# Reading the gate tiles ahead and moving two heads' scaling in a hybrid conv, gated linear attention and SwiGLU block

## The chip, the cores and the metric

The kernel runs on one core of one Trainium2 chip. The time is the device time of one execution in microseconds (us). Of the kernel before, three executions were timed, and one more was profiled. A difference of 0.2% is about 2.3 us here.

## The reference

`x` has 512 rows of 1024 values, in float32. One layer is computed:

```python
x = x + 0.5 * swiglu(rmsnorm(x, norm_ffn1_g), ffn1_w_gu, ffn1_w_down)
x = x + hybrid_mixer(rmsnorm(x, norm_mix_g), w_in, conv_w, ...)
x = x + 0.5 * swiglu(rmsnorm(x, norm_ffn2_g), ffn2_w_gu, ffn2_w_down)
return rmsnorm(x, final_norm_g)
```

The change touches the mixer:

```python
cb, cc, cu, q, k, v, g_lr, r, ga, gb = split(h @ w_in)
y_conv = (cb * causal_short_conv(cc * cu, conv_w)) @ w_out_conv
log_a = log_sigmoid(g_lr @ gate_w_up + gate_b) / 16
o = gla_chunked(q, k, v, log_a)                      # four heads, chunks of 64 rows
y_gla = (rmsnorm_of_each_head(o) * gla_norm_g * silu(r)) @ w_out_gla
merged = sigmoid(ga) * y_conv + sigmoid(gb) * y_gla
return merged @ w_o
```

`ga` and `gb` are the two gates, 512 x 1024 each. The attention is cut into chunks; in each, `q` and `k` are scaled by exponentials of cumulated decays, the scores are formed, a state is carried on, and the output is made of both.

## The kernel before, in words

**Products.** Each float32 weight tile is split into a high part (`wh`, a cast on ACT, L380) and the rest (`wl`, a subtraction on DVE, L381), and each operand likewise (L668, L669). A product takes three matmuls: high by high, high by low, low by high. The larger products are made by a scheme with seven half-size products in place of eight: the steps m1, p2, q6, p5, q7, p3 and p4. In a "tall" product (`Tall`, matmuls in L696) each step has two halves of 12 matmuls of 512 columns; in a "set" (`Set`, L613) a step has 24 matmuls of 256 columns. The program emits PE's instructions in a fixed order, step after step.

**Feeding PE.** `Weights.issue` (L351 to L389) is called some two steps ahead of PE. It loads the tiles of a step from HBM (SP's queue, L343, 512 KB, into 10 buffers `f`), adds tiles to one another where the scheme wants sums (DVE L359 and L374, or an accumulating DMA from POOL's queue, L347), and splits them into `wh` and `wl`, three buffers each. So a step can begin once its cast on ACT and its subtraction on DVE are done.

**Emptying PE.** Results stand in banks. A set has a bank "b" to which m1, q6, q7 and p4 add in turn; after m1, q6 and q7 it is copied out by ACT (L618), and the next of these steps can only begin to write it when that copy is done. A tall's banks are emptied by ACT (L1467) and DVE (L1469).

**The mixer.** PE takes `q`, `k`, then the tall products `v`, `ga`, `gb`, then eight sets (four for the convolution, 0 to 3; two for `cb`, 4 and 5; two for `r`, 6 and 7), then the tall product "out" (`w_out_conv`), `w_out_gla` (`mm_wide`, L449 to L451), and `w_o`. Each tile of `ga` and `gb` goes to HBM when it is made (L1484). The attention of the four heads is threaded between: a table `hooks` names after which step of PE each part of a head is emitted. The parts are `gates` (cumulated decays), `decays` (two subtractions, DVE L1336 and L1339), `exps` (ACT L1345 to L1349), `scale`, `scale_k`, `scale_q` (multiplications, all in the helper `mul`, DVE L583), `scores` (PE L1385, L1387, L1398), `state` (PE L1410, ACT L1412, DVE L1414), `output` (PE L1427 and L1430, ACT L1433 and L1435, DVE L1436) and `squares`. A hook gives the place in the program; the scheduler then orders DVE, ACT, POOL and SP by its own estimate of when things are ready. On each engine, instructions run strictly in that order, and one that waits holds all behind it.

**The gates' way back.** `gate(name, t, e)` (L1684) loads a gate tile (128 x 512, 256 KB, SP's queue, L1686) into one of the six buffers `tp` and takes its sigmoid on ACT (L1687). All sixteen loads stand around the `w_out_gla` product: `between(e)` multiplies the `ga` tiles into the conv output (DVE L583), and after each half of the product the `gb` tiles are multiplied with the banks and added (L583, L1726).

**Tiles that the change uses.** `E`, `M`, `KS`, `EX`, `QS` are the five work tiles of a head, `G_tile(0)` to `G_tile(4)`; `sc` holds the masked scores. `YS` holds the convolution's output in 1024-column quarters, `two(0)` to `two(3)`, and is read by the operands of "out" (`co`, L655, L668, L669).

**The start.** `WARM` matmuls of ones (L277) run on PE before the first weights and inputs have come; each is recorded as two matmuls.

Of the kernel before, what the change touches and what calls it, by code (L numbers as in the profile page):

```python
# [11 lines left out]
AF = mybir.ActivationFunctionType  # L12
# [15 lines left out]
NTB = S // P  # L28
# [6 lines left out]

V_G1, V_GM, V_G2, V_GLA, V_CONV, V_GB = 0, 8, 16, 24, 32, 56
NVEC = 60
WARM = 10
ODD_FILL = 272

TAIL = 4
# [191 lines left out]
def block_kernel(ctx: ExitStack, tc: tile.TileContext, xT, vecs, gf, gup, wgl, wts, out):  # L233
# [25 lines left out]
    def T(dtype=F32):  # L259
        return tile_of("tp", [P, S], dtype)  # L260
# [321 lines left out]
    def mul(out_, a, b, eng=None):  # L582
        (eng or nc.vector).tensor_tensor(out=out_, in0=a, in1=b, op=ALU.mult)  # L583
# [608 lines left out]
    def mixer(norm, nxt):  # L1192
# [15 lines left out]
        def two(i):  # L1208
            return flat(i).rearrange("p (e t) -> p e t", e=2)
# [6 lines left out]
        def G_tile(i, dtype=F32):  # L1216
            cnt[0] += 1
            return pools["g"].tile([P, S], dtype, tag=f"g{i}", name=f"g{i}_{cnt[0]}")
# [100 lines left out]
        def gates(h):  # L1319

            a = AUX()
            nc.tensor.matmul(a, gup_w[:R3, h * DK : (h + 1) * DK], glr[:R3],
                             start=True, stop=True)
            b = vec[:, V_GB + h : V_GB + h + 1]
            nc.scalar.activation(E, a, AF.Abs, bias=b)
            nc.vector.tensor_scalar(out=M, in0=a, scalar1=b, scalar2=0.0,
                                    op0=ALU.add, op1=ALU.min)
            nc.scalar.activation(E, E, AF.Exp, scale=-1.0)
            nc.scalar.activation(E, E, AF.Ln, bias=1.0)
            nc.vector.tensor_tensor(out=M, in0=M, in1=E, op=ALU.subtract)  # L1330
            nc.vector.tensor_tensor_scan(out=E, data0=reset, data1=M, initial=0.0,
                                         op0=ALU.mult, op1=ALU.add)
# [21 lines left out]
        def scale(h):  # L1354

            q_, k_ = QK[h][:, 0], QK[h][:, 1]
            ref = sm4[:, 0]
            mul(q_, EX, q_)  # L1360
            mul(KX, pairs(KS)[:, :, 0], pairs(k_)[:, :, 0])
            mul(QX, pairs(q_)[:, :, 1], bc(ref[:, :, 1]))

        def scale_k(h):

            k_, dc = QK[h][:, 1], sm4[:, 1]
            mul(pairs(KS)[:, :, 1], pairs(KS)[:, :, 1], pairs(k_)[:, :, 1])
            mul(k_, M, k_)
            mul(pairs(KS)[:, :, 0], KX, bc(dc[:, :, 1]))

        def scale_q(h):

            q_ = QK[h][:, 0]
            ref, dc = sm4[:, 0], sm4[:, 1]
            mul(pairs(QS)[:, :, 1], QX, bc(dc[:, :, 0]))
            mul(pairs(QS)[:, :, 0], pairs(q_)[:, :, 0], bc(ref[:, :, 0]))
            mul(d2s, dc[:, :, 0], dc[:, :, 1])

        def scores(h):
# [14 lines left out]
            n = NTB - 1  # L1394
            tr = AUX()
            for t in range(n):
                b = slice(t * P, (t + 1) * P)
                nc.tensor.transpose(tr[:, b], KS[:, b], ident)  # L1398
            nc.scalar.copy(E[:, : n * P], tr[:, : n * P])

        def state(h):

            v = vt[h // 2]
            kvs = []
            for t in range(NTB - 1):
                if t % 2 == 0:
                    kv = AUX()
                hc = slice((t % 2) * DV, (t % 2) * DV + DV)
                kvs.append(kv[:, hc])
                nc.tensor.matmul(kvs[t], E[:, t * P : (t + 1) * P],  # L1410
                                 v[t][:, (h % 2) * DV : (h % 2) * DV + DV], start=True, stop=True)
            nc.scalar.copy(ST[0], kvs[0])  # L1412
            for t in range(1, NTB - 1):
                nc.vector.scalar_tensor_tensor(out=ST[t], in0=ST[t - 1], scalar=d2s[:, t : t + 1],  # L1414
                                               in1=kvs[t], op0=ALU.mult, op1=ALU.add)
# [114 lines left out]
        def split_o(h):  # L1530
            for a, b in split_pair(O[h]):
                og_h.append(a)
                og_l.append(b)

        hooks = {
            ("v", 0, "q6"): [decays, exps], ("v", 1, "p5"): [lambda: scale(0)],
            ("v", 0, "q7"): [lambda: scale_k(0)],
# [1 line left out]
            ("ga", 1, "m1"): [lambda: state(0)], ("ga", 1, "p2"): [lambda: output(0)],  # L1539
            ("ga", 0, "p5"): [lambda: squares(0)], ("ga", 1, "p5"): [lambda: gates(1)],  # L1540
            ("ga", 0, "q7"): [decays], ("ga", 1, "q7"): [exps],
            ("ga", 0, "p3"): [lambda: scale(1)], ("ga", 1, "p3"): [lambda: scale_k(1)],
            ("gb", 0, "m1"): [lambda: scores(1)], ("gb", 1, "m1"): [lambda: scale_q(1)], ("gb", 0, "p2"): [lambda: state(1)],
            ("gb", 1, "q6"): [lambda: output(1)], ("gb", 1, "q7"): [lambda: squares(1)],
            ("gb", 0, "p3"): [move], ("gb", 1, "p3"): [lambda: gates(2)],
            ("gb", 0, "p4"): [decays], (0, "p2"): [exps], (0, "q6"): [lambda: scale(2)],
            (0, "p5"): [lambda: scale_k(2)], (0, "q7"): [lambda: scale_q(2)],
            (0, "p3"): [lambda: scores(2)], (1, "q6"): [lambda: state(2)],
            (1, "q7"): [lambda: output(2)], (1, "p4"): [lambda: squares(2)],
            (1, "p3"): [lambda: gates(3)], (2, "p5"): [decays], (2, "q7"): [exps],  # L1550
            (3, "m1"): [lambda: scale(3)], (2, "p4"): [lambda: scale_k(3)],
            (2, "p3"): [lambda: scale_q(3)],
            (3, "q6"): [lambda: scores(3)], (3, "p3"): [lambda: state(3)],
            (4, "q6"): [lambda: output(3)], (4, "p3"): [lambda: squares(3)],
            (5, "q7"): [lambda: normalise(0)], (5, "p3"): [lambda: normalise(1)],
            (6, "q7"): [lambda: normalise(2)], (6, "p3"): [lambda: normalise(3)],
            ("out", 1, "p5"): [lambda: co.make("p4")], ("out", 0, "q7"): [lambda: split_o(0)],
            ("out", 1, "q7"): [lambda: split_o(1)], ("out", 0, "p3"): [lambda: split_o(2)],
            ("out", 1, "p3"): [lambda: split_o(3)],
        }  # L1560
# [121 lines left out]
        finish_late()  # L1682

        def gate(name, t, e):  # L1684
            g = T()
            tc.keep_in_program_order(nc.sync.dma_start(g, gates_d[name][2 * t + e]))  # L1686
            nc.scalar.activation(g, g, AF.Sigmoid)  # L1687
            return g

# [17 lines left out]
        def between(e):  # L1707
            def extra(k):
                if e == 1 and k == 3:
                    XS.append(big("X2"))  # L1710
                    x[:] = [XS[-1][:, k] for k in range(KD)]
                    for k_ in range(KD):
                        nc.gpsimd.dma_start(x[k_], xs[k_])
                if k in (1, 3, 4, 6):
                    t = (1, 3, 4, 6).index(k)
                    mul(m[e][t], m[e][t], gate("ga", t, e))
                if e == 1 and k in (5, 6):
                    turned(2 * (k - 5))
            return extra
# [91 lines left out]
```

## Time and profile before

| what | value |
|---|---|
| executions, not profiled | 1168.29, 1169.42, 1169.52 us; median 1169.42 us |
| the profiled execution | 1169.12 us, of which the span of the profile is 1167.4 us |
| granted TensorE clock | 0.999 |
| busy: PE, DVE, ACT, POOL | 1158.9, 895.1, 657.3, 127.4 us |
| HBM read and written | 124.55 and 8.39 MB |
| DMA loads of weights (SP's queue) | 219 of 512 KB |

The profile's times are from the start of the span. In a row of the timeline stand the start, the length, engine, line, operation, output and inputs, and in brackets how long the engine had been idle and what ended that. DVE and ACT begin an instruction slightly ahead of the recorded end of the one before, so that the distance between two starts is the price of the first: 1.14 us for a subtraction L381 of 128 x 1024, 0.60 us for an operation of 128 x 512, 0.34 us for one of 128 x 256. PE's matmuls overlap in the records; the distance between starts, 0.227 us for 512 columns and 0.12 us for 256, is what one costs.

### The profile page before, as it was taken

How to read it: one execution, taken by the hardware profiler on the slowest of the kernel's cores; microseconds unless marked ns; L12 is line 12 of the kernel's file. 1: busy time of each engine (PE TensorE's matmuls, PEld its weight loads, DVE VectorE, ACT ScalarE, POOL GpSimd, SP SyncE). 2: the span in 40 equal slices, each digit the busy share in tenths (PEclk: the TensorE clock that was granted, in tenths of full speed). 3: DMA queues.
4: the chain of work that ended last, by engine and by line, in shares of the span. 5: the costliest groups of instructions: out<-in, count | busy, mean ns of one | idle time of the engine just before them, and what ended most of it. 6: DMA issues, size and time to landing. Idle time of an engine off the chain costs nothing.

```text
span 1167.4 us, 16527 instructions
## 1 busy us (share of the span) xinstructions
PE 1158.9 (99%) x6428; PEld 1010.3 (87%) x6428; DVE 895.1 (77%) x1066; ACT 657.3 (56%) x832; POOL 127.4 (11%) x167
## 2 busy tenths in 40 slices
PE   9999999999999999999999999999999999999997
PEld 7888888989988888889999998888888888888886
DVE  7985666889887976777797999555876666799966
ACT  6565555634452756475654577525655556575543
POOL 0101110001120110110110112000101101101100
PEclk9999999999999999999999999999999999999999
DMA  9667786657665485878576787834567966877711
GB/s 363 129 183 165 170 219 162 173 131 175 170 207 153 96 223 152 209 208 215 134 174 155 181 205 213 288 109 131 118 181 163 231 171 157 203 176 165 184 48 72
DMA packets 59870, 203.22 MB, mean 174 GB/s; under 512 B 6960, under 2 KB 7088, under 8 KB 59792
## 3 DMA queue, kind: packets, MB, share of 16 engines
q0 software_dynamic: 20288, 73.41, 33.3%
q1 hardware_dynamic: 36912, 124.27, 32.4%
q10 hardware_dynamic: 2592, 4.49, 1.0%
q8 instruction: 50, 0.82, 0.3%
q14 instruction: 28, 0.23, 0.1%
HBM read 124.55 MB, written 8.39 MB: 114 GB/s over the span
## 4 chain that ended last, share of the span: by engine, by line
PE 95%; DVE 2%; ACT 1%; DMA 1%; issue 0%; SPq 0%; ACTq 0%; DVEq 0%
PE mm L696 48%; PE mm L613 23%; PE mm L432 5%; PE mm L408 3%; PE mm L410 3%; PE mm L409 3%; PE aux L840 1%; PE mm L451 1%; PE mm L450 1%; PE mm L449 1%; PE mm L1083 1%; PE mm L1082 1%; PE mm L1081 1%; PE aux L1427 1%; DVE wl L381 1%
## 5 line engine op out<-in xcount | busy, mean ns | idle before, releaser
L380 ACT CAST wh<-f 128x1024 fp32r<-128x1024 f32 (+1 forms) x349 | 365.5, 1049 | 361.3 <-PE mm L696 138.0
L381 DVE TENSOR_TENSOR wl<-f,wh 128x1024 fp32r<-128x1024 f32 (+1 forms) x349 | 424.1, 1217 | 181.2 <-ACT wh L380 180.4
L696 PE MATMUL mm<-wh,op 128*128 128x512 f32 x1680 | 528.1, 391 | 0.0
L696 PEld LDWEIGHTS mm<-wh,op 128*128 128x128 f32 x1680 | 315.5, 188 | 65.8 <-ACT tp L814 0.8
L696 PE MATMUL mm<-wl,op 128*128 128x512 f32 x840 | 327.3, 390 | 0.2 <-DVE wl L381 0.2
L613 PE MATMUL mm<-op,wh 128*128 128x256 f32 x1456 | 263.7, 284 | 0.2 <-ACT tp L618 0.2
L613 PEld LDWEIGHTS mm<-op,wh 128*128 128x128 f32 x1456 | 227.0, 191 | 1.1 <-ACT tp L618 0.4
L347 POOL DMA_DIRECT2D f<-f x132 | 113.8, 865 | 910.5 <-DVE wl L381 434.1
L613 PE MATMUL mm<-op,wl 128*128 128x256 f32 x728 | 206.1, 283 | 0.3 <-DVE wl L381 0.3
L696 PEld LDWEIGHTS mm<-wl,op 128*128 128x128 f32 x840 | 157.8, 188 | 32.6 <-DVE wl L381 1.0
L613 PEld LDWEIGHTS mm<-op,wl 128*128 128x128 f32 x728 | 139.1, 191 | 0.5 <-DVE wl L381 0.5
L668 ACT CAST op<-hid 128x1024 fp32r<-128x1024 f32 x42 | 44.0, 1050 | 23.2 <-PE mm L696 11.0
L669 DVE TENSOR_TENSOR op<-hid,op 128x1024 fp32r<-128x1024 f32 x42 | 51.1, 1217 | 2.9 <-ACT op L668 2.9
L408 PE MATMUL mm<-op,wh 128*128 128x512 f32 x132 | 51.4, 389 | 0.0
L409 PE MATMUL mm<-op,wh 128*128 128x512 f32 x132 | 51.4, 389 | 0.0
L410 PE MATMUL mm<-op,wl 128*128 128x512 f32 x132 | 51.4, 389 | 0.0
L432 PE MATMUL mm<-op,wh 128*128 128x512 f32 x192 | 48.3, 393 | 0.3 <-ACT wh L380 0.2
L374 DVE TENSOR_TENSOR f<-f,f 128x1024 f32<-128x1024 f32 x30 | 36.6, 1220 | 10.9 <-DMA f<-f 8.6
L432 PEld LDWEIGHTS mm<-op,wh 128*128 128x128 f32 x192 | 35.6, 188 | 8.8 <-ACT wh L380 1.1
L408 PEld LDWEIGHTS mm<-op,wh 128*128 128x128 f32 x132 | 24.8, 188 | 5.2
L409 PEld LDWEIGHTS mm<-op,wh 128*128 128x128 f32 x132 | 24.8, 188 | 5.2
L410 PEld LDWEIGHTS mm<-op,wl 128*128 128x128 f32 x132 | 24.8, 188 | 5.1
(326 smaller groups left out, 1194.8 us busy)
## 6 DMA issues: line engine op xcount, KB each, us to landing
f<-wts SPq DMA_DIRECT2D x219, 512.0 KB, 4.3
f<-f POOLq DMA_DIRECT2D x132, 512.0 KB, 5.1
X<-xT SPq DMA_DIRECT2D x8, 256.0 KB, 5.7
xs<-X POOLq DMA_DIRECT2D x8, 256.0 KB, 2.8
ga<-tp ACTq DMA_DIRECT2D x8, 256.0 KB, 5.2
gb<-tp ACTq DMA_DIRECT2D x8, 256.0 KB, 3.9
tp<-ga SPq DMA_DIRECT2D x8, 256.0 KB, 5.1
X<-xs POOLq DMA_DIRECT2D x8, 256.0 KB, 7.3
```

The source lines that it names most:

```text
L347: nc.gpsimd.dma_start(out_, a, accum_op=ALU.add)
L374: nc.vector.tensor_tensor(out=a11, in0=a11, in1=a22, op=ALU.subtract)
L380: nc.scalar.copy(h[:, :w], raw[:, :w])
L381: nc.vector.tensor_tensor(out=l[:, :w], in0=raw[:, :w], in1=h[:, :w].bitcast(F32), op=ALU.subtract)
L408: nc.tensor.matmul(o, wh, ah, start=first, stop=False)
L409: nc.tensor.matmul(o, wh, al, start=False, stop=False)
L410: nc.tensor.matmul(o, wl, ah, start=False, stop=last)
L432: nc.tensor.matmul(o[c], w[:, s : s + P], a[k], start=k == 0 and j == 0, stop=k == kt - 1 and j == 2)
L613: nc.tensor.matmul(to, ww[:, s], aa[:, t], start=fresh and k == 0 and e == 0 and j == 0, stop=k == 3 and j == 2, skip_group_check=True)
L668: nc.scalar.copy(hv, v)
L669: nc.vector.tensor_tensor(out=lv, in0=v, in1=hv.bitcast(F32), op=ALU.subtract)
L696: nc.tensor.matmul(self.bank[b][e], aa[:, c], ww, start=fresh and i == 0 and n == 0, stop=k == 3 and n == 2, skip_group_check=True)
```

## The change

Four things are changed.

1. **Four `ga` tiles of the first half** (e = 0) are loaded into `KS`, `EX`, `QS` and `sc` after the first half of m1 of "out" in the program (`fetch_gates`), and their sigmoid is taken after q6 (`open_gates`). The scheduler puts these loads further ahead, to where head 3 has read these tiles for the last time.
2. **Eight more** (`gb` of e = 0, `ga` of e = 1) are loaded into the quarters of `YS` within "out" (`fetch_more`); `gate` then takes a tile from there. The four `gb` tiles of e = 1 go through `tp` as before.
3. **Heads 1 and 3**: some of `decays`, `exps`, `scale`, `scale_k`, `scale_q`, `scores` and `state` hang on a later step.
4. `WARM` is 9 in place of 10.

```diff
-WARM = 10
+WARM = 9
...
+        ahead = {}
+        def fetch_gates():
+            for t, g in enumerate((G_tile(2), G_tile(3), G_tile(4), sc)):
+                nc.sync.dma_start(g, gates_d["ga"][2 * t])
+                ahead[t] = g
+        def open_gates():
+            for t in range(NTB):
+                nc.scalar.activation(ahead[t], ahead[t], AF.Sigmoid)
+        def fetch_more(name, e):
+            for t in range(NTB):
+                g = two(2 * e + t // 2)[:, t % 2]
+                nc.sync.dma_start(g, gates_d[name][2 * t + e])
+                ahead[name, t, e] = g
...
-            ("ga", 0, "p3"): [lambda: scale(1)], ("ga", 1, "p3"): [lambda: scale_k(1)],
+            ("ga", 1, "p3"): [lambda: scale(1)], ("ga", 1, "p4"): [lambda: scale_k(1)],
...
+            ("out", 0, "m1"): [fetch_gates], ("out", 1, "q6"): [open_gates],
+            ("out", 0, "q7"): [lambda: split_o(0), lambda: fetch_more("gb", 0)],
+            ("out", 0, "p4"): [lambda: fetch_more("ga", 1)],
...
         def gate(name, t, e):
-            g = T()
-            tc.keep_in_program_order(nc.sync.dma_start(g, gates_d[name][2 * t + e]))
+            g = ahead.get((name, t, e))
+            if g is None:
+                g = T()
+                tc.keep_in_program_order(nc.sync.dma_start(g, gates_d[name][2 * t + e]))
             nc.scalar.activation(g, g, AF.Sigmoid)
             return g
...
-                    mul(m[e][t], m[e][t], gate("ga", t, e))
+                    mul(m[e][t], m[e][t], ahead[t] if e == 0 else gate("ga", t, e))
```

The order that the scheduler makes of it is shown at three places. In the rows, the numbers are buffers; `g_536` to `g_540` are `E`, `M`, `KS`, `EX`, `QS`; the change's buffers are numbered one lower.

**DVE, head 1**, where `ga` ends and `gb` begins; `y` holds this head's `q` and `k`. Before:

```order
L381 TENSOR_TENSOR wl_4201<-f_3801,wh_4200 128x1024
L583 TENSOR_TENSOR y_3223<-g_539_3456,y_3223 128x512
L583 TENSOR_TENSOR g_538_3455<-g_538_3455,y_3223 128x4x64
L583 TENSOR_TENSOR g_539_3456<-g_538_3455,y_3223 128x256
L583 TENSOR_TENSOR g_539_3456<-y_3223,sm 128x256
L381 TENSOR_TENSOR wl_4221<-f_3851,wh_4220 128x1024
L1469 SCALAR_TENSOR_TENSOR tp_4082<-mm_4086,tp_4082 128x512
L1469 SCALAR_TENSOR_TENSOR tp_4084<-mm_4087,tp_4084 128x512
L583 TENSOR_TENSOR y_3223<-g_537_3454,y_3223 128x512
L583 TENSOR_TENSOR g_538_3455<-g_539_3456,sm 128x4x64
L381 TENSOR_TENSOR wl_4244<-f_4143,wh_4243 128x1024
```

The same place in the change:

```order
L381 TENSOR_TENSOR wl_4200<-f_3800,wh_4199 128x1024
L583 TENSOR_TENSOR y_3222<-g_539_3455,y_3222 128x512
L583 TENSOR_TENSOR g_538_3454<-g_538_3454,y_3222 128x4x64
L381 TENSOR_TENSOR wl_4217<-f_3850,wh_4216 128x1024
L1469 SCALAR_TENSOR_TENSOR tp_4081<-mm_4085,tp_4081 128x512
L1469 SCALAR_TENSOR_TENSOR tp_4083<-mm_4086,tp_4083 128x512
L583 TENSOR_TENSOR g_539_3455<-g_538_3454,y_3222 128x256
L583 TENSOR_TENSOR g_539_3455<-y_3222,sm 128x256
L381 TENSOR_TENSOR wl_4240<-f_4142,wh_4239 128x1024
L583 TENSOR_TENSOR y_3222<-g_537_3453,y_3222 128x512
L381 TENSOR_TENSOR wl_4258<-f_4191,wh_4257 128x1024
```

The second L381 now stands ahead of two 128 x 256 multiplications, and the third ahead of the multiplication of `k` and of one more 128 x 256.

**DVE, head 3**, in the last convolution set; `y` is the convolution's, `vec` its weights. Before:

```order
L1579 SCALAR_TENSOR_TENSOR tp_5308<-y_3223,vec,tp_5308 128x512
L1581 SCALAR_TENSOR_TENSOR y_3223<-y_3223,vec,tp_5304 128x512
L1581 SCALAR_TENSOR_TENSOR y_3223<-y_3223,vec,tp_5308 128x512
L1336 TENSOR_TENSOR g_537_3454<-g_536_3453 128x512
L1339 TENSOR_TENSOR g_538_3455<-g_536_3453 128x512
L381 TENSOR_TENSOR wl_5323<-f_4786,wh_5322 128x1024
L1593 SCALAR_TENSOR_TENSOR tp_5352<-mm_5274,tp_5350 128x512
L381 TENSOR_TENSOR wl_5361<-f_5042,wh_5360 128x1024
```

In the change, whose lines are numbered 21 higher here:

```order
L1600 SCALAR_TENSOR_TENSOR tp_5307<-y_3222,vec,tp_5307 128x512
L1602 SCALAR_TENSOR_TENSOR y_3222<-y_3222,vec,tp_5303 128x512
L1602 SCALAR_TENSOR_TENSOR y_3222<-y_3222,vec,tp_5307 128x512
L381 TENSOR_TENSOR wl_5320<-f_4785,wh_5319 128x1024
L1336 TENSOR_TENSOR g_537_3453<-g_536_3452 128x512
L1339 TENSOR_TENSOR g_538_3454<-g_536_3452 128x512
L1614 SCALAR_TENSOR_TENSOR tp_5349<-mm_5273,tp_5347 128x512
L381 TENSOR_TENSOR wl_5355<-f_5041,wh_5354 128x1024
```

The two subtractions of `decays` went behind one L381; the next L381 has the same work ahead of it as before.

**ACT, after head 3's output.** `O` and `aux` are the head's output and its bank, `tp` what is copied out of a set's bank. Before:

```order
L1433 ACTIVATE O<-aux_5792,vec 128x512
L1435 ACTIVATE g_538_3455<-aux_5792 128x512
L380 CAST wh_5849<-f_5320 128x1024
L380 CAST wh_5883<-f_5579 128x1024
L618 COPY tp_5877<-mm_5617 128x512
L380 CAST wh_5914<-f_5316 128x1024
```

In the change, where L1544 is `open_gates`:

```order
L1433 ACTIVATE O<-aux_5791,vec 128x512
L1435 ACTIVATE g_538_3454<-aux_5791 128x512
L1544 ACTIVATE sc<-sc 128x512
L380 CAST wh_5848<-f_5317 128x1024
L1544 ACTIVATE g_997_6690<-g_997_6690 128x512
L1544 ACTIVATE g_995_6688<-g_995_6688 128x512
L380 CAST wh_5882<-f_5578 128x1024
L618 COPY tp_5876<-mm_5616 128x512
L380 CAST wh_5913<-f_5313 128x1024
```

Three sigmoids (`sc`; `g_997`, which is `QS`'s tile; `g_995`, which is that of `KS`) now stand among the casts and copies of the sets, each behind its load. The fourth, in the tile of `EX`, stands some steps earlier, together with a load of ACT's function table.

More of the change, by code (lines that the diff above doesn't have):

```diff
@@ L1541, in mixer @@
             ("ga", 0, "q7"): [decays], ("ga", 1, "q7"): [exps],
-            ("ga", 0, "p3"): [lambda: scale(1)], ("ga", 1, "p3"): [lambda: scale_k(1)],
-            ("gb", 0, "m1"): [lambda: scores(1)], ("gb", 1, "m1"): [lambda: scale_q(1)], ("gb", 0, "p2"): [lambda: state(1)],
+            ("ga", 1, "p3"): [lambda: scale(1)], ("ga", 1, "p4"): [lambda: scale_k(1)],
+            ("gb", 1, "m1"): [lambda: scores(1)], ("gb", 0, "p2"): [lambda: scale_q(1)],
+            ("gb", 1, "p2"): [lambda: state(1)],
             ("gb", 1, "q6"): [lambda: output(1)], ("gb", 1, "q7"): [lambda: squares(1)],
@@ L1549, in mixer @@
             (1, "q7"): [lambda: output(2)], (1, "p4"): [lambda: squares(2)],
-            (1, "p3"): [lambda: gates(3)], (2, "p5"): [decays], (2, "q7"): [exps],
-            (3, "m1"): [lambda: scale(3)], (2, "p4"): [lambda: scale_k(3)],
+            (1, "p3"): [lambda: gates(3)], (2, "q7"): [decays], (3, "m1"): [exps],
+            (2, "p4"): [lambda: scale(3)], (3, "p2"): [lambda: scale_k(3)],
             (2, "p3"): [lambda: scale_q(3)],
@@ L1556, in mixer @@
             (6, "q7"): [lambda: normalise(2)], (6, "p3"): [lambda: normalise(3)],
-            ("out", 1, "p5"): [lambda: co.make("p4")], ("out", 0, "q7"): [lambda: split_o(0)],
+            ("out", 0, "m1"): [fetch_gates], ("out", 1, "q6"): [open_gates],
+            ("out", 1, "p5"): [lambda: co.make("p4")],
+            ("out", 0, "q7"): [lambda: split_o(0), lambda: fetch_more("gb", 0)],
+            ("out", 0, "p4"): [lambda: fetch_more("ga", 1)],
             ("out", 1, "q7"): [lambda: split_o(1)], ("out", 0, "p3"): [lambda: split_o(2)],
```

## The prediction

> **What bounds the kernel now.** I read the page first, then PE's waits, then the busy time by stage, then the timeline of PE and DVE around each wait. The page's busy times:
>
> ```profile
> PE 1158.9 (99%) x6428; PEld 1010.3 (87%) x6428; DVE 895.1 (77%) x1066; ACT 657.3 (56%) x832; POOL 127.4 (11%) x167
> ```
>
> PE is idle for 1167.4 - 1158.9 = 8.5 us of the span, and a part of that is the start and the tail after the last product. A change that leaves PE its products can therefore win only what PE waits for. The view of waits, for PE, names three in the middle of the program (the first number is the total in us):
>
> ```profile
> PE mm L613 <- DVE wl L381: 0.3, 1, 0.3
> PE mm L696 <- DVE wl L381: 0.2, 1, 0.2
> ...
> PE mm L613 <- ACT tp L618: 0.2, 1, 0.2
> ```
>
> Two are for a `wl` from DVE, one for a copy by ACT. The busy time by stage, for "out" and then for the `w_out_gla` product (start:end, length, then busy us of PE, PEld, DVE, ACT and POOL):
>
> ```profile
> 697.20:735.30 38.10, 38.10 (x170) 31.54 (x169) 34.92 (x36) 26.73 (x31) 6.88 (x11) 1.00 0.83 246
> 735.30:773.40 38.10, 38.10 (x170) 31.49 (x169) 17.88 (x21) 16.39 (x23) 0.00 (x0) 1.00 0.64 221
> ```
>
> PE is busy for all of both. The gate tiles stand in the second stage now and in the first and before it afterwards; no wait of PE stands where they are taken away.
>
> **Head 1's scaling.** The timeline of PE, then of DVE, where `ga` passes into `gb`:
>
> ```profile
> 474.05 0.61 PE L696 MATMUL mm<-wh,op 128*128 128x512 f32 x2
> ...
> 474.73 0.61 PE L696 MATMUL mm<-wh,op 128*128 128x512 f32 x2
> ...
> 475.92 0.62 PE L696 MATMUL mm<-wh,op 128*128 128x512 f32 x2
> ```
>
> ```profile
> 469.44 0.68 DVE L583 TENSOR_TENSOR y<-g,y 128x512 f32<-128x512 f32 x1
> 470.04 0.75 DVE L583 TENSOR_TENSOR g<-g,y 128x256 f32<-128x256 f32 x2
> 470.71 0.41 DVE L583 TENSOR_TENSOR g<-y,sm 128x256 f32<-128x256 f32 x1
> 471.05 1.21 DVE L381 TENSOR_TENSOR wl<-f,wh 128x1024 fp32r<-128x1024 f32 x1
> 472.19 1.27 DVE L1469 SCALAR_TENSOR_TENSOR tp<-mm,tp 128x512 f32<-128x512 f32 x2
> 473.38 0.67 DVE L583 TENSOR_TENSOR y<-g,y 128x512 f32<-128x512 f32 x1
> 473.98 0.41 DVE L583 TENSOR_TENSOR g<-g,sm 128x256 f32<-128x256 f32 x1
> 474.32 1.21 DVE L381 TENSOR_TENSOR wl<-f,wh 128x1024 fp32r<-128x1024 f32 x1
> 475.46 0.41 DVE L583 TENSOR_TENSOR g<-g,sm 128x256 f32<-128x256 f32 x1
> 475.79 1.21 DVE L381 TENSOR_TENSOR wl<-f,wh 128x1024 fp32r<-128x1024 f32 x1
> ```
>
> Three products normally take 474.73 - 474.05 = 0.68 us; from 474.73 to 475.92 they take 1.19. That is 0.51 us lost, on the third L381, which ends at 474.32 + 1.21 = 475.53 while PE wants it at 474.73 + 0.45 = 475.18. In the new order the multiplication of `k` (473.38 to 473.98, 0.60) and one 128 x 256 (473.98 to 474.32, 0.34) stand behind it: it starts at 474.32 - 0.94 = 473.38 and ends at 474.59, 0.6 us early. The banks that the L1469 ahead of it empty were filled by a step that PE had ended well before, so they can move up 0.67 us with it. Gain: **0.51 us**. What is late next is the L381 at 475.79: nothing new stands ahead of it, it ends by 477.00, and PE's next step (12 products of 0.227, 2.72 us) wants it at 475.18 + 2.72 = 477.90. It hides.
>
> One price stands against it: `scores` and `state` of head 1 come a half-step later, and on DVE two evacuations and an L381 now stand ahead of the second L1414, which makes the state for the output. Its rows, DVE's and PE's:
>
> ```profile
> 493.39 0.47 DVE L1414 SCALAR_TENSOR_TENSOR stt<-g,d,aux 128x256 f32<-128x256 f32 x1
> ```
>
> ```profile
> 496.49 0.39 PE L1430 MATMUL aux<-g,stt 128*128 128x128 f32 x2
> ```
>
> It ended at 493.86 and was wanted at 496.49, a reserve of 2.63, less the 0.51 by which PE now comes earlier: 2.12. Ahead of it come 1.20 for two evacuations and 1.14 for one L381, together 2.34. So up to 0.22 us is lost again, or nothing if DVE, which has idle time there, gets to this work sooner. I take 0.1, half way: the two ends lie close together.
>
> **Head 3's scaling.** PE, then DVE, in the last convolution set:
>
> ```profile
> 585.49 0.40 PE L613 MATMUL mm<-op,wh 128*128 128x256 f32 x2
> ...
> 586.42 0.40 PE L613 MATMUL mm<-op,wh 128*128 128x256 f32 x2
> ...
> 586.78 0.40 PE L613 MATMUL mm<-op,wh 128*128 128x256 f32 x2
> ```
>
> ```profile
> 583.73 0.68 DVE L1336 TENSOR_TENSOR g<-g 128x512 f32<-128x512 f32 x1
> 584.33 0.68 DVE L1339 TENSOR_TENSOR g<-g 128x512 f32<-128x512 f32 x1
> 584.93 1.21 DVE L381 TENSOR_TENSOR wl<-f,wh 128x1024 fp32r<-128x1024 f32 x1
> ...
> 586.67 1.21 DVE L381 TENSOR_TENSOR wl<-f,wh 128x1024 fp32r<-128x1024 f32 x1
> ```
>
> Three products take 0.36 us (586.42 to 586.78), the three before took 0.93: 0.57 us lost. The two subtractions of `decays` (1.20) now stand behind the L381, which so ends at 586.14 - 1.20 = 584.94, while PE wants it at 585.49 + 0.24 = 585.73. Gain: **0.57 us**. Next is the L381 at 586.67, with the same work ahead as before: it ends at 587.88 and is wanted one step (24 products of 0.12, 2.88 us) after 585.73, at 588.61. It hides.
>
> **The gate tiles: nothing won, and a price to bound.** On SP, three of the four early loads wait for head 3's output and the sum of its squares (DVE L1436, below), and the weights queue behind them. On ACT, the sigmoids stand among casts and copies, and hold them until their tile has landed. ACT, DVE and PE around head 3's output:
>
> ```profile
> 629.99 1.05 ACT L380 CAST wh<-f 128x1024 fp32r<-128x1024 f32 x1 [1.83 <-PE mm L613]
> 630.94 0.58 ACT L618 COPY tp<-mm 128x512 f32<-128x512 f32 x1
> ```
>
> ```profile
> 626.38 0.69 DVE L1436 TENSOR_TENSOR g<-g,g 128x512 f32<-128x512 f32 x1
> ```
>
> ```profile
> 632.75 0.40 PE L613 MATMUL mm<-op,wh 128*128 128x256 f32 x2
> ```
>
> The last of the three tiles, in the place of `KS`, can be asked for at 626.38 + 0.69 = 627.07. Behind its sigmoid come that cast (0.95 to the next start) and the copy of the set's bank (0.58), and at 632.75 PE adds to this bank again. The sigmoid's length, 0.63, and the table load of 1.28 us that one of them brings along are seen where they stand now:
>
> ```profile
> 722.98 1.28 ACT L1687 ACT_TABLE_LOAD   x1
> 724.27 0.63 ACT L1687 ACTIVATE tp<-tp 128x512 f32<-128x512 f32 x1
> ```
>
> So the tile must land by 632.75 - 0.58 - 0.95 - 0.63 = 630.59, which is 3.5 us after the request; later costs PE the difference. How long such transfers took: the weights' loads from 619 to 634 us (count, size, median us to landing), and all transfers of `ga`:
>
> ```profile
> f<-wts SPq DMA_DIRECT2D x2, 512.0 KB, 3.5
> ```
>
> ```profile
> DMA to landing us min/median/max: 2.0/5.1/8.5
> ```
>
> The price lies between 0 (2.0 us) and 8.5 - 3.5 = 5.0 us. I take 0: the first row is of this very stretch and of twice the size, while the second includes the transfers that crowd in the `w_out_gla` stage. The same holds for SP: the tile leaves the queue at about 627.4, and the weights behind it land as soon as they did in 3.5 us, with a step's reserve. The tiles in `YS` wait likewise within "out", where DVE's reading of `YS` ends before the weights behind need their buffers; if that cover is gone, the price is of the same kind.
>
> The Trainium skill (ScalarE: Activation LUTs, What ACT_TABLE_LOAD costs) puts a switch of tables at 2.66 us, 1.38 of it a drain. The two rows show 1.29 us from the load to the activation, so the measurement decides; by the Trainium skill's figure, ACT would be held 1.4 us longer at one place, which I estimate at no more than 0.2 us of PE's time, and the sum would be 0.8 in place of 1.0.
>
> **Nine warming products.** PE's busy time at the start (two records for each product), and the first real products:
>
> ```profile
> 1.10:4.30 3.20, 3.19 (x15) 1.00 0.69 236
> 4.40:4.88 0.48, 0.48 (x7) 1.00 0.91 333
> ```
>
> ```profile
> 5.06 1.17 PE L432 MATMUL mm<-op,wh 128*128 128x512 f32 x4
> ```
>
> Fifteen records start within the first 3.2 us, 0.21 us apart, and the last five within 0.48 us (two of the seven had begun before), 0.1 us apart. Two fewer end the warming 0.22 us sooner, at about 4.65 in place of 4.87; the first real product starts at 5.06 in both, since it waits for its inputs and not for PE: 0.
>
> **Sum.** 0.51 + 0.57 - 0.1 = 0.98, rounded to 1.0 us. The profiled execution took 1169.12 us and would take 1168.1; the median of the runs, 1169.42, lies 0.3 above it, so I forecast **1168.4 us**. A measurement tells about 0.2%, 2.34 us, from no change: faster means below 1167.08, slower above 1171.76.
>
> **Rivals.**
>
> *Given back.* The waits move to another L381, to the state of head 1, or to a copy a little late. For it: DVE is busy 77% and the reserves above are 0.6 to 0.9 us. Against: each next one was followed. Time: 0.2 to 1.1 us lost again, about 1169.2.
>
> *Slower: ACT is held by a sigmoid.* Place: the tile of `KS`, behind which the copy of the bank stands. It decides from a landing time of 3.5 us. At the median of `ga`, 5.1, PE loses 1.6 us (1170.0, still within 0.2%); at the longest, 8.5, it loses 5.0 us: 1168.4 + 5.0 = **1173.4 us**. Slower by over 0.2% takes 3.36 us, a landing of 6.9 us. For it: PE already waits once for such a copy (L618 in the view of waits). Against: the row of 3.5 us.
>
> *The clock.* The products run at half rate until 4.4 us, 3.3 us after the first. If the shorter warming let the full rate begin only after 3.3 us of real products, some 12 of them (four take 0.91 us at full rate) would each cost 0.227 us more: 2.7 us, 1171.1. The trace speaks against it: the rate rises before the ninth product ends. By the Trainium skill (TensorE: Matmul & The Clock Gate, Part 1: The HAM clock gate), the full clock comes after about 3.4 us of sustained work in a window that runs freely, so the moment may differ from run to run; the 3.3 us here agree.
>
> *More goes.* The wait for L618 goes too, 0.2 us or somewhat more: 1168.0. To be faster by 0.2%, twice the two gains would be needed, and PE's view of waits has no such time.
>
> **How the numbers follow.** Chances: forecast 0.60, given back 0.19, slower 0.06, clock 0.04, more goes 0.07, and 0.04 for a gain that the profile doesn't show. Below 1167.08 falls only the last, with the edge of the runs' spread: 0.05. Above 1171.76 falls the slower case and the edge of the clock's: 0.07. Within: 0.88. The three runs before lie 1.23 us apart, so a median may be off by about 0.6. Low end: 1168.0 - 0.6, and 0.4 for waits shorter than the view's limit: 1167.0. High end: nothing gained, 1169.4, and 0.6, and 0.2 of the median landing's price: 1170.2.
>
> **What would show it.** Right: in the profile after, no wait of PE for `wl` at head 1 and head 3, PE busy throughout "out" and `w_out_gla`, ACT's waits for gate tiles in the `w_out_gla` stage mostly gone, and a span near 1166.4. Wrong: a wait of PE for L618 at head 3's output behind an L1544 sigmoid (slower), a wait for L1414 before head 1's output or for the next L381 (given back), real products 0.45 us apart at the start (clock), or a span that falls by more than 2 us.

## The result, and the profile after

| what | before | after |
|---|---|---|
| median of 11 executions each, not profiled | 1169.28 us | 1171.42 us |
| the profiled execution | 1169.12 us | 1172.33 us |
| its span | 1167.4 us | 1170.6 us |
| busy: PE, DVE, ACT | 1158.9, 895.1, 657.3 us | 1159.7, 895.0, 658.9 us |

The changed kernel is slower by 2.1 us: the ratio is 1.0023, with a 95% interval of 1.0013 to 1.0032. The forecast was 1168.4 us, within 0.2%, and its range ended at 1170.2. The engines do the same work as before; so PE must wait somewhere new. Of all executions below, one, of the kernel before with nine warming products, took 1937.88 us at a granted clock of 0.556, and its ratio leaves it out. The view of PE's waits, after (total in us, times, longest):

```profile
PE mm L613 <- ACT tp L618: 1.8, 2, 1.6
...
PE mm L696 <- DVE wl L381: 0.8, 1, 0.8
...
PE mm L696 <- ACT wh L380: 0.2, 1, 0.2
```

The 0.3 us of L613 for L381, which belonged to head 3, are gone. For L618 there was one wait of 0.2 us; now there are two, of 1.8 us in all. The 0.8 and 0.2 of L696 stand at another place than head 1's wait.

**Heads 1 and 3.** DVE at head 1, then PE there and at head 3, after:

```profile
473.84 0.41 DVE L583 TENSOR_TENSOR g<-y,sm 128x256 f32<-128x256 f32 x1
474.18 1.21 DVE L381 TENSOR_TENSOR wl<-f,wh 128x1024 fp32r<-128x1024 f32 x1
475.31 0.68 DVE L583 TENSOR_TENSOR y<-g,y 128x512 f32<-128x512 f32 x1
```

```profile
475.51 0.62 PE L696 MATMUL mm<-wh,op 128*128 128x512 f32 x2
...
476.19 0.62 PE L696 MATMUL mm<-wh,op 128*128 128x512 f32 x2
```

```profile
585.74 0.40 PE L613 MATMUL mm<-op,wh 128*128 128x256 f32 x2
...
586.10 0.40 PE L613 MATMUL mm<-op,wh 128*128 128x256 f32 x2
```

PE stands 0.8 us later at head 1 than before, for a reason that lies at the start (below), so the products of 474.73 and 475.92 in the kernel before are those of 475.51 and 476.19 here. The third L381 now stands ahead of the multiplication of `k`, and three products take their 0.68 and 0.36 us without a break. Both waits are gone, 0.51 and 0.57 us.

**Head 3's output.** ACT, then PE, after; the brackets give the idle time ahead and what ended it:

```profile
626.76 0.63 ACT L1544 ACTIVATE sc<-sc 128x512 f32<-128x512 f32 x1 [1.11 <-DMA sc<-ga]
627.29 1.03 ACT L380 CAST wh<-f 128x1024 fp32r<-128x1024 f32 x1
630.05 0.63 ACT L1544 ACTIVATE g<-g 128x512 f32<-128x512 f32 x1 [1.72 <-DMA g<-ga]
632.13 0.63 ACT L1544 ACTIVATE g<-g 128x512 f32<-128x512 f32 x1 [1.45 <-DMA g<-ga]
632.67 1.03 ACT L380 CAST wh<-f 128x1024 fp32r<-128x1024 f32 x1
633.60 0.58 ACT L618 COPY tp<-mm 128x512 f32<-128x512 f32 x1
```

```profile
632.31 0.28 PE L613 MATMUL mm<-op,wl 128*128 128x256 f32 x1
634.23 0.50 PE L613 MATMUL mm<-op,wh 128*128 128x256 f32 x2 [1.65 <-ACT tp L618]
```

Each of the three sigmoids waits for its tile, 4.3 us in all. Behind the last, in the tile of `KS`, stand the cast and the copy of the set's bank, and PE stands still from 632.31 to 634.23: 1.92 us in place of 0.12, a loss of 1.80. The two products that start there take 0.34 us to the next start in place of 0.24, which makes 1.90.

**In "out".** ACT, PE and the gate tiles' transfers:

```profile
712.59 1.28 ACT L1710 ACT_TABLE_LOAD   x1 [3.45 <-DMA y<-gb]
713.88 0.63 ACT L1710 ACTIVATE y<-y 128x512 f32<-128x512 f32 x1
714.42 1.98 ACT L380 CAST wh<-f 128x1024 fp32r<-128x1024 f32 x2
```

```profile
714.88 0.39 PE L696 MATMUL mm<-wh,op 128*128 128x512 f32 x1
715.51 0.51 PE L696 MATMUL mm<-wh,op 128*128 128x512 f32 x1 [0.24 <-ACT wh L380]
716.77 0.50 PE L696 MATMUL mm<-wl,op 128*128 128x512 f32 x1 [0.76 <-DVE wl L381]
717.10 0.63 PE L696 MATMUL mm<-wh,op 128*128 128x512 f32 x2
```

```profile
DMA to landing us min/median/max: 4.7/5.0/5.3
```

The same thing a second time: ACT waits 3.45 us for the first tile in `YS`, loads its function table only then, and two casts come late, the subtraction on DVE with them. PE loses 0.40, 1.03 and 0.10 us (the three distances less 0.23 each), 1.54 us.

The account: 1.90 + 1.54 lost, 1.08 won, makes 2.36 us, beside 2.14 between the medians. The profiled executions differ by more, 3.2 us; the rest, 0.8 us, arises before 30 us, and the experiments with nine and ten warming products bear on it.

### The profile page after: what moved, and what is told of

Its sections match the earlier page's. It is cut to its first block, busy times and chain, and to the rows that moved or that the text cites. A ratio compares the mean times of both kernels' runs of the same rounds, so it can differ in the third digit from the quotient of the medians.

```text
span 1170.6 us, 16516 instructions
## 1 busy us (share of the span) xinstructions
PE 1159.7 (99%) x6426; PEld 1010.7 (86%) x6426; DVE 895.0 (76%) x1066; ACT 658.9 (56%) x833; POOL 127.3 (11%) x167
## 4 chain that ended last, share of the span: by engine, by line
PE 96%; DMA 2%; ACT 1%; DVE 1%; issue 0%; SPq 0%; ACTq 0%; DVEq 0%
PE mm L696 48%; PE mm L613 23%; PE mm L432 5%; PE mm L409 3%; PE mm L408 3%; PE mm L410 3%; PE aux L840 1%; PE mm L451 1%; PE mm L449 1%; PE mm L450 1%; PE mm L1083 1%; PE mm L1082 1%; PE mm L1081 1%; PE aux L1427 1%; PE aux L1430 0%; DMA X<-xT 0%
## 5 line engine op out<-in xcount | busy, mean ns | idle before, releaser
L380 ACT CAST wh<-f 128x1024 fp32r<-128x1024 f32 (+1 forms) x349 | 365.1, 1048 | 365.0 <-PE mm L696 136.7
L381 DVE TENSOR_TENSOR wl<-f,wh 128x1024 fp32r<-128x1024 f32 (+1 forms) x349 | 424.5, 1219 | 187.3 <-ACT wh L380 186.6
L696 PE MATMUL mm<-wh,op 128*128 128x512 f32 x1680 | 528.6, 391 | 0.2 <-ACT wh L380 0.2
L696 PEld LDWEIGHTS mm<-wh,op 128*128 128x128 f32 x1680 | 315.5, 188 | 66.4 <-ACT tp L814 0.8
L696 PE MATMUL mm<-wl,op 128*128 128x512 f32 x840 | 327.4, 390 | 0.8 <-DVE wl L381 0.8
L613 PE MATMUL mm<-op,wh 128*128 128x256 f32 x1456 | 263.8, 284 | 1.8 <-ACT tp L618 1.8
L613 PEld LDWEIGHTS mm<-op,wh 128*128 128x128 f32 x1456 | 227.3, 192 | 2.9 <-ACT tp L618 2.2
L613 PE MATMUL mm<-op,wl 128*128 128x256 f32 x728 | 206.0, 283 | 0.0
L696 PEld LDWEIGHTS mm<-wl,op 128*128 128x128 f32 x840 | 157.8, 188 | 33.2 <-DVE wl L381 1.7
L613 PEld LDWEIGHTS mm<-op,wl 128*128 128x128 f32 x728 | 139.4, 191 | 0.0
```

Source lines behind the costliest of these rows:

```text
L380: nc.scalar.copy(h[:, :w], raw[:, :w])
L381: nc.vector.tensor_tensor(out=l[:, :w], in0=raw[:, :w], in1=h[:, :w].bitcast(F32), op=ALU.subtract)
L613: nc.tensor.matmul(to, ww[:, s], aa[:, t], start=fresh and k == 0 and e == 0 and j == 0, stop=k == 3 and j == 2, skip_group_check=True)
L696: nc.tensor.matmul(self.bank[b][e], aa[:, c], ww, start=fresh and i == 0 and n == 0, stop=k == 3 and n == 2, skip_group_check=True)
```

## The experiments

Two theories. The first: ACT stands at sigmoids whose tile has not landed, and holds the copy and the casts that PE waits for. The rival: the early loads themselves cost the time, by delaying weights on SP's queue or by taking the transfers' rate. A third question is the start. The kernel before was run again beside each group and took 1169.50 to 1169.67 us; each ratio is against those runs. The changed kernel's 1171.42 us stands beside its own runs of before, at 1169.28.

### The moves of heads 1 and 3 alone

```diff
-            ("out", 0, "m1"): [fetch_gates], ("out", 1, "q6"): [open_gates],
-            ("out", 0, "q7"): [lambda: split_o(0), lambda: fetch_more("gb", 0)],
-            ("out", 0, "p4"): [lambda: fetch_more("ga", 1)],
+            ("out", 0, "q7"): [lambda: split_o(0)],
...
-WARM = 9
+WARM = 10
```

> Only the moves of heads 1 and 3 are made; no gate tile is read ahead and ten warming products stay. If the two waits for L381 are really won (0.51 and 0.57 us), the time is 1.0 to 1.1 us below the kernel before, about 1168.2 us, and PE waits neither at 474 nor at 585 us. If what is won there is lost again later (at head 1's state L1414, or at the next L381), the time is that of before, 1169.3 us, and a new wait of PE shows where. If the moves themselves carry a part of the loss of the whole change (2.1 us), it is above 1169.5 us.

1168.31 us beside 1169.52, ratio 0.9992 (0.9983 to 1.0001). Of all PE's waits for L618, L380 and L381, one is left, which stood in the kernel before too:

```profile
PE mm L613 <- ACT tp L618: 0.2, 1, 0.2
```

So in this profile the 1.1 us are won and not given back. The interval just reaches 1: by the times alone so small a gain is hardly told from none; the trace tells it.

### The whole change, each sigmoid kept where its tile is used

```diff
-            ("out", 0, "m1"): [fetch_gates], ("out", 1, "q6"): [open_gates],
+            ("out", 0, "m1"): [fetch_gates],
...
-            nc.scalar.activation(g, g, AF.Sigmoid)
+            tc.keep_in_program_order(nc.scalar.activation(g, g, AF.Sigmoid))
```

> The whole change, with the twelve loads where they are in it, but each sigmoid of a gate tile is kept at the place where the tile is used, in the w_out_gla stage; nothing of the computation changes. If PE lost its time because ACT stood at sigmoids whose tile had not landed, and held the copy L618 (1.9 us at 632 us) and two casts L380 (1.54 us at 715 us), both losses go, and the time is 3.4 us below the changed kernel's 1171.4, about 1168.0 us. If instead the loads themselves cost the time, by delaying the weights behind them on SP's queue or by taking the transfers' rate, the losses stay, and the time is within 0.7 us of 1171.4.

1167.67 us beside 1169.52, ratio 0.9985 (0.9976 to 0.9993). ACT around head 3's output, where the loads are issued as in the change:

```profile
625.78 1.05 ACT L380 CAST wh<-f 128x1024 fp32r<-128x1024 f32 x1 [1.15 <-issue]
628.66 1.05 ACT L380 CAST wh<-f 128x1024 fp32r<-128x1024 f32 x1 [1.83 <-PE mm L613]
629.61 0.58 ACT L618 COPY tp<-mm 128x512 f32<-128x512 f32 x1
```

SP and POOL issue their transfers in the same order as in the change, and the tiles of `KS` and `QS` still take 5.7 us to land (median). But the cast waits for PE again, not PE for ACT, and both losses are gone with the loads still there. The first theory holds, and the rival falls: the loads cost nothing, the place of the sigmoids does.

### Only the tile of `KS` not read ahead

```diff
-            for t, g in enumerate((G_tile(2), G_tile(3), G_tile(4), sc)):
+            for t, g in ((1, G_tile(3)), (2, G_tile(4)), (3, sc)):
...
-                    mul(m[e][t], m[e][t], ahead[t] if e == 0 else gate("ga", t, e))
+                    mul(m[e][t], m[e][t], ahead[t] if e == 0 and t else gate("ga", t, e))
```

> The whole change, but the gate tile in KS is not read ahead; it goes through a free tile in the w_out_gla stage as before. The three others of the first four, and the eight in YS, stay. If the wait for KS's tile alone is what delays the copy L618 at 632 us, the 1.9 us there go, or all but 0.3 us of them (QS's tile landed at 630.0, and sigmoid, cast and copy behind it take 2.1 us), while the 1.5 us at 715 us stay: about 1169.6 us. If the wait moves to QS's sigmoid, or the weights' landing is what counts, more than 1 us stays at 632 us: 1170.5 us or more.

1169.80 us beside 1169.61, ratio 1.0002 (0.9993 to 1.0011). ACT, then PE in "out":

```profile
628.40 0.63 ACT L1544 ACTIVATE g<-g 128x512 f32<-128x512 f32 x1 [1.65 <-DMA g<-ga]
628.93 1.03 ACT L380 CAST wh<-f 128x1024 fp32r<-128x1024 f32 x1
629.87 0.58 ACT L618 COPY tp<-mm 128x512 f32<-128x512 f32 x1
630.92 1.05 ACT L380 CAST wh<-f 128x1024 fp32r<-128x1024 f32 x1 [0.48 <-PE mm L613]
```

```profile
712.12 0.50 PE L696 MATMUL mm<-wh,op 128*128 128x512 f32 x1 [0.34 <-ACT wh L380]
713.38 0.50 PE L696 MATMUL mm<-wl,op 128*128 128x512 f32 x1 [0.76 <-DVE wl L381]
```

`QS`'s sigmoid still waits 1.65 us for its tile, but the copy behind it is in time, and the loss at head 3's output is gone altogether. That in "out" stays. So the waits of ACT cost by their place: of the three sigmoids, the last alone reached PE.

### Only the four tiles in `KS`, `EX`, `QS` and `sc` read ahead

```diff
-            ("out", 0, "q7"): [lambda: split_o(0), lambda: fetch_more("gb", 0)],
-            ("out", 0, "p4"): [lambda: fetch_more("ga", 1)],
+            ("out", 0, "q7"): [lambda: split_o(0)],
```

> The whole change without the eight tiles in YS; the four in KS, EX, QS and sc stay. If the two losses have one cause each, 1.9 us at 632 us stay and the 1.5 us at 715 us go: about 1169.9 us. If the eight loads in YS have nothing to do with 715 us, the time is that of the changed kernel, 1171.4.

1169.66 us beside 1169.61, ratio 1.0001 (0.9993 to 1.0010), and the mirror image in PE's waits: no wait of L696 is left, and L613 keeps its own.

```profile
PE mm L613 <- ACT tp L618: 1.9, 2, 1.7
```

Each loss goes with its own loads, and each alone is more than the 1.1 us that the heads win.

### The function table loaded ahead of the wait

```diff
+        def table():
+            tc.keep_in_program_order(nc.scalar.activation(sm[:, 0, 0:1], sm[:, 0, 0:1], AF.Sigmoid))
...
-            ("out", 0, "m1"): [fetch_gates], ("out", 1, "q6"): [open_gates],
+            ("out", 0, "m1"): [fetch_gates, table], ("out", 1, "q6"): [open_gates],
```

> The whole change, and one sigmoid of a single column that nothing reads, early in the out product, so that ACT's function table is loaded before the first tile in YS has landed. It stands at 712.59 in the changed kernel, behind a wait of 3.45 us for that tile. If the table's load waits for the tile only because the sigmoid behind it does, its 1.28 us now lie under the wait, and PE loses 0.3 to 0.9 us at 715 us in place of 1.54 (the scheduler now also puts two sigmoids, not one, ahead of the first cast): about 1170.6 us. If the tile's landing alone sets the wait, 1.5 us stay.

1172.63 us beside 1169.61, ratio 1.0022 (1.0013 to 1.0032). ACT in "out", and the tiles' landing:

```profile
699.33 1.28 ACT L1547 ACT_TABLE_LOAD   x1
...
708.51 0.63 ACT L1713 ACTIVATE y<-y 128x512 f32<-128x512 f32 x1 [1.03 <-DMA y<-gb]
712.52 0.63 ACT L1713 ACTIVATE y<-y 128x512 f32<-128x512 f32 x1 [3.37 <-DMA y<-gb]
713.06 1.03 ACT L380 CAST wh<-f 128x1024 fp32r<-128x1024 f32 x1
```

```profile
DMA to landing us min/median/max: 3.5/6.9/7.3
```

PE has a wait here that the changed kernel doesn't have:

```profile
721.68 0.50 PE L696 MATMUL mm<-wl,op 128*128 128x512 f32 x1 [0.53 <-DVE wl L381]
```

The table is out of the way, but two sigmoids now stand ahead of the first cast, and the tiles take 6.9 us to land (median) in place of 5.0; why they do isn't shown. At the first cast PE loses as much as before (1.57 us), and at 721.68 it loses 0.8 us more. The time came out 2 us above the 1170.6 that was expected if the table's load counted. Since the order and the landing changed along with the table, this one decides nothing on the table's share: by the durations, 1.28 of the 1.54 us could be the table's, which is an estimate and not shown.

### The accumulating transfers beside the tiles cut to 8 columns

Why did the tiles take over 5 us, where weights of twice the size took 3.5? In both stretches an accumulating transfer of 512 KB from POOL's queue was under way. Three of these were cut, with the order of all instructions unchanged.

```diff
-            nc.gpsimd.dma_start(out_, a, accum_op=ALU.add)
+            nc.gpsimd.dma_start(out_[:, :(8 if self.issued in (189, 214, 215) else 1024)], a[:, :(8 if self.issued in (189, 214, 215) else 1024)], accum_op=ALU.add)
```

> The whole change, its instructions in the same order, but three of the accumulating transfers of weights (L347), those in flight beside the gate tiles at 623, 703 and 706 us, add 8 columns in place of 1024; so the output is made with three incomplete weight sums, and only the time counts. If these transfers stretch the landing of the gate tiles (KS 5.3 us, QS 5.8, the first in YS 5.0), these land in 3 to 3.5 us, ACT is free in time, and both losses of PE go, 1.9 us at 632 and 1.5 at 715: about 1168.0 us. If the landing depends on SP's queue or on the tiles' own transfers, it stays above 5 us, and the time is that of the changed kernel, 1171.4. In between, each microsecond of landing beyond 3.5 costs PE one at 632 us.

1167.82 us beside 1169.67, ratio 0.9988 (0.9979 to 0.9998). The transfers around head 3's output (count, KB each, median us to landing), in the changed kernel and here:

```profile
f<-f POOLq DMA_DIRECT2D x1, 512.0 KB, 6.2
g<-ga SPq DMA_DIRECT2D x2, 256.0 KB, 5.5
```

```profile
g<-ga SPq DMA_DIRECT2D x2, 256.0 KB, 2.8
...
f<-f POOLq DMA_DIRECT2D x1, 4.0 KB, 3.5
```

ACT here, where the last sigmoid's tile was asked for at 625.2:

```profile
627.87 0.63 ACT L1544 ACTIVATE g<-g 128x512 f32<-128x512 f32 x1 [0.69 <-DMA g<-ga]
628.41 1.03 ACT L380 CAST wh<-f 128x1024 fp32r<-128x1024 f32 x1
629.34 0.58 ACT L618 COPY tp<-mm 128x512 f32<-128x512 f32 x1
```

The tiles land in half the time, and both losses are gone, although every sigmoid is where the change has it. (A wait of 0.5 us for L381 at 903 us, in a part that the change does not touch, stands in this profile alone.)

### The same three transfers as plain copies

```diff
-            nc.gpsimd.dma_start(out_, a, accum_op=ALU.add)
+            nc.gpsimd.dma_start(out_, a, **({} if self.issued in (189, 214, 215) else {"accum_op": ALU.add}))
```

> The whole change, its instructions in the same order, but the same three transfers of weights as in small sums keep their 1024 columns and only copy in place of adding; so the output is made with three wrong weight sums, and only the time counts. With 8 columns, the tiles in KS and QS landed in 2.8 us (median) in place of 5.5, and both losses went. If it is the bytes beside them that stretch the landing, a copy of 512 KB does it as well: 5 us, and about 1171.4 us. If it is the adding, the tiles land in 3 to 3.5 us, and the time is about 1168 us.

1167.76 us beside 1169.50, ratio 0.9988 (0.9979 to 0.9997). The two tiles' landing, then ACT and PE; the `KS` tile was asked for at 625.1:

```profile
g<-ga SPq DMA_DIRECT2D x2, 256.0 KB, 4.0
```

```profile
629.24 0.63 ACT L1544 ACTIVATE g<-g 128x512 f32<-128x512 f32 x1 [1.12 <-DMA g<-ga]
```

```profile
630.66 0.28 PE L613 MATMUL mm<-op,wl 128*128 128x256 f32 x1
631.34 0.50 PE L613 MATMUL mm<-op,wh 128*128 128x256 f32 x2 [0.40 <-ACT tp L618]
```

By the profile, this is neither of the two expected ends, but between them: PE still loses 0.56 us at head 3's output, and nothing in "out". The times alone don't tell it from the kernel with 8 columns (1167.82 us). With the last request and the last sigmoid's start, the three kernels make a series for the tile of `KS`:

| the transfer ahead | landing of `KS` | PE's loss at the copy |
|---|---|---|
| 8 columns added | 627.87 - 625.2 = 2.7 us | 0 |
| 512 KB copied | 629.24 - 625.1 = 4.1 us | 0.56 us |
| 512 KB added | 632.13 - 626.8 = 5.3 us | 1.80 us |

In both last rows, landing less loss is 3.5 us: the point from which the prediction let its slower rival decide. The rows differ in more than the adding, though. The copy itself landed after 3.8 us, at about 625.5, just after the tile was asked for; the addition took 6.2 us, to about 629.6, and was in flight beside the tile for 2.8 us. And in the last row the next load of weights was asked for at 629.61, 2.5 us before the tile had landed.

### Nine and ten warming products

Two kernels change nothing but `WARM`: the changed kernel with ten, and the kernel before with nine.

```diff
-WARM = 9
+WARM = 10
```

> The whole change, with ten warming products as before. PE reaches 425 us 0.80 us later in the profile of the changed kernel than before. If nine warming products bring that, the time is 0.5 to 0.8 us below the changed kernel's, about 1170.7 us, and the offset at 425 us is within 0.2 us of none. If it is the landing of the second x tile, which differs from run to run, the time is that of the changed kernel, 1171.4 us, and the first products' times go with that landing.

```diff
-WARM = 10
+WARM = 9
```

> The kernel before, with nine warming products in place of ten and nothing else. If the ninth alone carries the 0.80 us at the start, the time is 0.5 to 0.8 us above the kernel before, about 1169.9 us. If not, it is that of before, 1169.3 us.

With ten, the changed kernel took 1173.02 us beside 1169.52, ratio 1.0035 (1.0023 to 1.0047, 6 executions), no less than with nine; the kernel before with nine took 1169.60 beside 1169.52, ratio 1.0004 (0.9995 to 1.0013). The third kernel is the one with late sigmoids, with ten:

> The kernel with late sigmoids, and ten warming products. In the three profiles with nine, the fifth real product starts 1.45 to 1.69 us after the first, with ten it starts 1.01 after it. If these 0.4 to 0.7 us reach the end, the time is 0.4 us below that of late sigmoids, about 1167.3 us. If the later waits for x and the weights swallow them, it is the same, 1167.7.

1167.91 us beside 1169.61, ratio 0.9984 (0.9974 to 0.9993), as with nine. The first eight real products in the kernel before, and in it with nine warming products:

```profile
5.06 2.09 PE L432 MATMUL mm<-op,wh 128*128 128x512 f32 x8
```

```profile
5.04 2.66 PE L432 MATMUL mm<-op,wh 128*128 128x512 f32 x8
```

With nine, these take 0.57 us longer here, and nothing is left of it further on: the 103rd real product starts at 28.88 us there, and at 29.34 in the kernel before. The 0.8 us at the start of the changed kernel's profiled execution belong to that execution: its 103rd real product starts at 30.14, that of the same kernel with ten warming products at 29.15. Over all thirteen profiles this start lies between 28.50 and 30.14 with nine, and between 28.51 and 30.24 with ten. It goes with the landing of an `x` tile, for which ACT waits ahead of its first operands (L484): that row stands at 5.16 us in the kernel with the earliest start, 6.36 in the kernel before, 7.13 in the changed one and 7.24 in the one with the latest.

### The reads alone, with late sigmoids

The heads and `WARM` are as in the kernel before; only the twelve loads stand ahead.

```diff
-            g = T()
-            tc.keep_in_program_order(nc.sync.dma_start(g, gates_d[name][2 * t + e]))
-            nc.scalar.activation(g, g, AF.Sigmoid)
+            g = ahead.get((name, t, e))
+            if g is None:
+                g = T()
+                tc.keep_in_program_order(nc.sync.dma_start(g, gates_d[name][2 * t + e]))
+            tc.keep_in_program_order(nc.scalar.activation(g, g, AF.Sigmoid))
```

> The kernel before, with the twelve tiles read ahead as in the change and every sigmoid kept where its tile is used; heads 1 and 3 and the ten warming products are as before. If reading ahead brings PE nothing, because PE waits for no gate tile in the kernel before, the time is that of before, 1169.6 us. If the early loads themselves bring something, by leaving the w_out_gla stage fewer transfers, it is 0.4 to 0.6 us below, about 1169.1, which is what the two kernels with late sigmoids lie below the one with the moved heads alone. If they delay weights, it is above 1170.

1169.29 us beside 1169.67, ratio 1.0000 (0.9991 to 1.0009). Reading ahead brings nothing. ACT's waits for gate tiles in the `w_out_gla` stage, before and in the changed kernel:

```profile
ACT tp L1687 <- DMA tp<-ga: 7.6, 4, 2.8
ACT tp L1687 <- DMA tp<-gb: 5.3, 3, 3.4
```

```profile
ACT tp L1710 <- DMA tp<-gb: 4.5, 1, 4.5
```

They fall from 12.9 to 4.5 us, as the change would have it, but PE never waited for them.

## Why the prediction was wrong, point by point

- **Head 1's and head 3's scaling, 0.51 + 0.57 us:** right in mechanism, place and size; the moves alone gave 1.2 us by the medians, at the edge of what the times tell, and both waits are gone in every profile with the moves.
- **Given back at head 1's state, 0.1 us:** nothing. The second L1414 started at 495.32, later than its 493.39 of before, and the product that reads it started at 496.74 without a wait.
- **The gate tiles bring nothing:** right, by the kernel with the reads alone.
- **The gate tiles cost nothing: this step failed.** The prediction named the place, the sigmoid in `KS`'s tile with the copy of the bank behind it, and the point, a landing of 3.5 us. It then took the landing from the row of the weights' loads, 3.5 us, "of this very stretch and of twice the size", and gave the slower case 6 in 100. The landing was 5.3 us, near the 5.1 of the row that it set aside, and the loss 1.80 us, where it had reckoned 1.6 for 5.1. What the row of 3.5 us left out is what else is in flight. The view of transfers of before lists an accumulating transfer beside these loads, but not in flight with them: the two loads were asked for at 620.03 and 629.44 and landed after 3.6 and 3.4 us, the addition was asked for at 623.67 and landed after 4.6, and so ran between them. The three early tiles are asked for while the addition is in flight (it at 623.35, they from 623.80 to 626.8), and the kernel with 8 columns shows that it stretches the landing. That 5.1 came so near is in part luck: that row is of other loads, at 720 to 745 us, and of stores at 444 to 477.
- **The tiles in `YS`: the same step failed a second time,** in one sentence. "The price is of the same kind" was never worked out. The weights' buffers, on which it rested, were not the point; ACT's order was: one sigmoid ahead of two casts, behind a landing of 5 us and a table's load, whose price is 1.29 us from its start to the activation here too (712.59 to 713.88). It cost 1.54 us. The two prices together, 1.90 and 1.54 us, turn 1.1 us won into 2.4 lost by the trace, 2.1 by the medians.
- **Nine warming products, 0:** held in the time, and half in its reason. The first real product did start as before, at 5.07 us. But the warming ended no sooner: its last record starts at 4.89 us in place of 4.87, since with nine its records kept the slow distance of 0.21 us to the end. And the first products ran slower with nine, by 0.3 us or more in six of eight profiles, as the clock's rival had it, though for four products at most and not for twelve; by the 103rd nothing of it is seen.

The slower rival was thus right about its mechanism, and its 1.6 us at a landing of 5.1 were near the 1.80 measured at its place. What it lacked was the second place, and a chance that wasn't drawn from the wrong row. The version that beats both kernels is the change with late sigmoids: 1167.67 us, 0.15% below the kernel before (0.07% to 0.24%), and by the two ratios, 0.9985 and 1.0023, 0.4% below the changed one.

## What to carry to other kernels

In these runs, loads put ahead cost nothing as long as the instruction that waits for them did not come ahead as well: on an engine that works in order, as ACT does in the rows above, an early consumer holds everything behind it until the tile lands. Where a scheduler places that consumer, look in the order for what stands behind it, and work out by when the tile must land. Take the landing time from transfers with the same neighbours in flight, and where two rows differ, price the longer one.

## What the runs showed of the hardware

- An accumulating transfer stretched the landing of the tiles beside it, in most cases more than a copy of the same 512 KB did. At head 3's output, `KS` landed in 5.3 us beside the addition, 4.0 with the copy and 2.6 with 8 columns (the table above counts to the sigmoid's start), `QS` in 5.8, 4.1 and 3.1, but `sc`, asked for first, in 2.9, 3.8 and 2.9. In "out", the median of the first four tiles was 5.0, 3.6 and 3.1. The addition also takes longer to land itself (6.2 us, the copy 3.8), so how much comes of the adding and how much of the longer time in flight stays open. The Trainium skill (Collectives: The Full Stack, The bandwidth ceiling: the fold count and why AG ≠ RS ≠ AR) says of a collective that adds, ReduceScatter, that it is slow because the add reads two sources, not because of the arithmetic. No run here shows whether that is the reason for these transfers too.
- The load of ACT's function table waits with the activation that it stands before: it began at 712.59 us, when the tile of the sigmoid behind it had landed, after 3.45 us in which ACT had nothing else to do.
- The pace of the first products differs between executions: with nine warming products the fifth started 1.00 to 1.83 us after the first in eight profiles, with ten about 1.01 in four and 1.30 in one. The granted clock is 1.00 in the rows of the first 10 us of all of them, so the slower pace isn't seen in it.
